# Rearranging the two front halves of an encoder layer: a gates piece moved to the short attention, two query heads to a bank, the second picks among gathers, the first query products ahead of the last transposes

## The chip, the cores and the metric

One NeuronCore of a Trainium2 chip runs the whole kernel in one launch. The metric is the device time of one execution in microseconds (us), and of several executions the median. The engines are TensorE (PE: matrix products and transposes; PEld in the profile is its loading of weights, which overlaps), VectorE (DVE), ScalarE (ACT), GpSimd (POOL) and SyncE (SP, which here only issues transfers).

## The reference

One encoder layer is computed for two sequences with the same weights: a prompt of 256 tokens, called "p" in the kernel, and a sample of 512 tokens, called "s". Everything is fp32.

```python
h = rms_norm(x, norm1)
proj = h @ w_in                                  # 1024 -> 5120 columns
qa, ka, va, qb, kb, vb, ga, gb = split(proj)
ya = banded_attention(rope(qa), rope(ka), va, sink) @ w_o_a       # 8 heads, 2 kv heads
ob = softmax-weighted sum of three dilated attentions of 4 heads each
yb = ob @ w_o_b
x = x + (sigmoid(ga) * ya + sigmoid(gb) * yb) @ w_out
t = rms_norm(x, norm2)                           # then the expert part, "peer"
q = (t @ w_query).reshape(T, 8 heads, 2, 128)
s1, s2 = scores of q against 128 + 128 sub-keys of each head
top 16 of s1, top 16 of s2, top 16 of their 256 sums  -> idx (128 experts a token), g
x = x + sum_e g_e * gelu(expert_u[idx_e] . t) * expert_v[idx_e]   # of 16384 experts
```

## The kernel before

**Products.** fp32 operands are split into two parts (`hi`, made by a cast on ScalarE, and `lo`, the rest, made by a subtraction on VectorE or GpSimd: `split`), and each product is three matmuls into the same bank of PSUM (`mm3`: hi by hi, hi by lo, lo by hi). Weights come through `w_stream` in pairs of 128x512 blocks: 512 KB into `wraw` (two buffers, issued by SP), a cast to `whi`, a subtraction to `wlo` (three buffers each). The table `LP` says which pairs are subtracted on GpSimd (`onpool`).

**The front of a sequence** (`front`), of nt = 2 tiles of 128 tokens for p and 4 for s, is in order: the norm and its transposes (`norm1`); six chunks of `w_in` (chunk c = 4 first, then 0, 1, 2, 3, 5), after each of which `post` norms and rotates queries and keys on VectorE and transposes them (`p_qk`), running along the next chunk's products; the attention (`att`), with 8 + 4 + 4 heads per tile; `merge`, which transposes the attention's outputs `on` (`p_toT<-ident,on`, split into `oTh` and `oTl`) and multiplies by `w_o_a` and `w_o_b` (`pya`, `pyb`); `w_out` (`pwo`, whose second half runs in two halves of the tiles, `proj_halves`); per tile `done`: the residual add, the norm, and the transposes of `xn` into `tTh` and `tTl` (`to_T`); and four chunks of `w_query` (`pq`, four heads of 128 columns each), whose results are copied (`qT`), scored against the keys (`p_s`) and reduced to the 16 best by `top16` on VectorE. The first query chunk of s is done for tokens 0:256 first and then for 256:512.

**Fillers.** The sigmoid gates' columns of `w_in` are computed in eight pieces (`PIECES`, `gates_pre`: for s 96 matmuls `pg` of 128x256 and two transfers of 512 KB a piece), and they fill the attention, where TensorE would wait for softmaxes. `along(att(), more, rate)` deals a piece's steps out among the attention's. In p's attention the filler `more` is s's first norm, p's own eight pieces, and those s pieces that `GS` puts there; `GS` also puts some behind p's `w_out`, and the rest fill s's attention.

**The prompt's experts** run beside everything else. `front("p")` runs alone. Then `fill(front("s"), gg, ...)` advances a chain `gg` by FILL = 2.25 steps for each unit that the front yields (a yield's number of units is written in the code; `IPW` is that of a pair of weights of s's projection, `MU` that of the other projections). The chain begins with the prompt's picks, `pick`, 11 steps for each of two tiles: candidates, 16 top-8 searches, and four rounds of `eq`, `pr`, `ex` (a compare, a product and a sum of 1600 elements a partition) on VectorE, ending in the table of expert numbers `pidx`. Then come the gathers, `gather`: for each tile 128 steps over `expert_u` and 128 over `expert_v`, in each of which GpSimd issues a transfer of 128 rows of 4 KB by `pidx` into `gr` and VectorE takes one product with it (`gr<-gr,tok` or `x<-gr,act,x`). There are 512 such steps. They go on beside the sample's dense expert part: `stage1` (all 16384 `expert_u` products, `pu`), `gbuild` (the sample's gates), `stage2` (all `expert_v` products, `held`). What is left of the chain at the end is run by itself.

**What sets the order.** Within an engine the instructions stand in an order that a scheduler writes down before the run, by priorities that follow the order in which the code issues them; where it expects a wait, it takes what comes later. On the chip each engine runs its list in order. So a step that the code moves takes with it everything that the scheduler places around it. The PSUM banks of the front are in four pairs: `mm` and `mb` for products (a `half` of 0 or 1), `tr` and `o` for transposes and attention outputs.

## Time and profile before

| | before |
|---|---|
| median of three runs | 2438.69 us (2438.09 to 2441.15) |
| the profiled execution: own time, span | 2441.6 us, 2439.8 us |
| TensorE busy, mean granted clock | 2332.6 us (96% of the span), 0.981 |
| VectorE busy | 1880.8 us (77%) |
| ScalarE busy | 1073.6 us (44%) |
| GpSimd busy | 830.0 us (34%) |

The profile is of one execution; the span runs from its first to its last instruction, and its own time is 1.8 us more. A wait is shown as the idle time ahead of an instruction, with the instruction that ended it. The granted clock is that of TensorE as a share of full speed. Names such as `wlo` or `gr` are the tiles of the code, with their numbers left out. Instructions of a front's helper all have the helper's line: L145 to L147 are the three matmuls of `mm3`, L243 to L245 those of a gates piece, L166 the transposes of `to_T`, L141 the subtraction of `split`, L813 the gather's product over `expert_u`, L821 that over `expert_v`.

### The profile page before, as it was taken

What the parts mean: (1) busy time and instruction counts of PE and PEld (TensorE: products, weight loads), DVE (VectorE), ACT (ScalarE), POOL (GpSimd) and SP (SyncE); (2) the same over time, 40 slices, a digit from 0 to 9 for tenths busy, and PEclk for the clock granted to TensorE, in tenths of its full rate; (3) what the DMA queues carried; (4) which work ended last, traced back from release to release, by engine and by line L of the source; (5) the groups of instructions that cost most, each with busy time, mean ns of one, the idle gap of its engine ahead of it and who ended that gap; (6) DMA issues with size and microseconds to landing.
All of it is one profiled execution on the core that took longest, in us unless ns stands there. A gap on an engine that the chain in (4) does not pass through costs nothing.

```text
span 2439.8 us, 34171 instructions
## 1 busy us (share of the span) xinstructions
PE 2332.6 (96%) x11926; PEld 1958.4 (80%) x11926; DVE 1880.8 (77%) x4013; ACT 1073.6 (44%) x1848; POOL 830.0 (34%) x624
## 2 busy tenths in 40 slices
PE   7998998999997999999999999998899999999996
PEld 5787986877977888888888888887688888888885
DVE  6765699687698889978577888771588787878787
ACT  5664444543433334366466667642333232222231
POOL 0000320255555500145244444440333344444443
PEclk9999999999998999999999999999899999999998
DMA  6423542477788434479789999893999999999997
GB/s 214 149 87 121 181 136 70 147 231 221 274 301 268 130 109 136 153 271 345 282 294 337 323 337 363 336 341 129 389 373 348 357 355 370 350 334 395 353 363 265
DMA packets 246365, 642.79 MB, mean 263 GB/s; under 512 B 22576, under 2 KB 77488, under 8 KB 244144
## 3 DMA queue, kind: packets, MB, share of 16 engines
q1 hardware_dynamic: 151728, 305.02, 36.7%
q0 software_dynamic: 73728, 268.47, 30.5%
q10 hardware_dynamic: 20736, 67.12, 6.9%
q8 instruction: 94, 1.54, 0.3%
q14 instruction: 79, 0.65, 0.1%
HBM read 561.60 MB, written 77.59 MB: 262 GB/s over the span
## 4 chain that ended last, share of the span: by engine, by line
PE 77%; DMA 8%; DVE 7%; issue 3%; ACT 2%; POOL 2%; SPq 0%; POOLq 0%; ACTq 0%; DVEq 0%
PE held L145 10%; PE held L146 9%; PE held L147 9%; PE pu L147 9%; PE pu L146 9%; PE pu L145 9%; PE p_g L725 5%; DMA wraw<-w_in 3%; DMA gr<-u,pidx 2%; PE pg L245 1%; PE pg L244 1%; DVE wlo L141 1%; POOL wlo L141 1%; PE pg L243 1%; ACT whi L140 1%
## 5 line engine op out<-in xcount | busy, mean ns | idle before, releaser
L806 POOL DMA_INDIRECT gr<-u,pidx x256 | 329.7, 1288 | 588.2 <-ACT ph L140 262.8
L806 POOL DMA_INDIRECT gr<-v,pidx x256 | 353.4, 1381 | 462.6 <-ACT ph L140 187.7
L145 PE MATMUL held<-vh,ph 128*128 128x512 f32 x1024 | 399.1, 391 | 17.5 <-ACT ph L140 17.5
L813 DVE SCALAR_TENSOR_TENSOR gr<-gr,tok 128x1024 f32<-128x1024 f32 x256 | 331.1, 1300 | 103.3 <-DMA gr<-u,pidx 103.2
L145 PE MATMUL pu<-tTh,uh 128*128 128x512 f32 x1024 | 406.2, 397 | 0.7 <-ACT uh L140 0.7
L147 PE MATMUL pu<-tTh,ul 128*128 128x512 f32 x1024 | 398.9, 390 | 0.6 <-DVE ul L141 0.6
L146 PE MATMUL pu<-tTl,uh 128*128 128x512 f32 x1024 | 399.2, 390 | 0.0
L146 PE MATMUL held<-vl,ph 128*128 128x512 f32 x1024 | 397.9, 390 | 0.0
L821 DVE SCALAR_TENSOR_TENSOR x<-gr,act,x 128x1024 f32<-128x1024 f32 x256 | 328.2, 1282 | 68.2 <-DMA gr<-v,pidx 66.4
L147 PE MATMUL held<-vh,pl 128*128 128x512 f32 x1024 | 332.4, 389 | 0.0
L141 POOL TENSOR_TENSOR wlo<-wraw,whi 128x1024 fp32r<-128x1024 f32 x51 | 126.0, 2472 | 376.0 <-ACT whi L140 369.2
L141 DVE TENSOR_TENSOR vl<-vr,vh 128x1024 fp32r<-128x1024 f32 x128 | 156.2, 1223 | 113.2 <-ACT vh L140 112.8
L145 PEld LDWEIGHTS held<-vh,ph 128*128 128x128 f32 x1024 | 193.2, 189 | 58.2 <-ACT ph L140 18.1
L140 ACT CAST uh<-ur 128x1024 fp32r<-128x1024 f32 x128 | 134.3, 1050 | 238.9 <-PE pu L146 127.4
L147 PEld LDWEIGHTS pu<-tTh,ul 128*128 128x128 f32 x1024 | 192.5, 188 | 41.3 <-DVE ul L141 1.1
L146 PEld LDWEIGHTS held<-vl,ph 128*128 128x128 f32 x1024 | 192.8, 188 | 40.2
L147 PEld LDWEIGHTS held<-vh,pl 128*128 128x128 f32 x1024 | 192.2, 188 | 40.0
L145 PEld LDWEIGHTS pu<-tTh,uh 128*128 128x128 f32 x1024 | 192.9, 188 | 38.3 <-ACT uh L140 1.1
L146 PEld LDWEIGHTS pu<-tTl,uh 128*128 128x128 f32 x1024 | 192.8, 188 | 37.2
L140 ACT CAST ph<-gl 128x512 fp32r<-128x512 f32 x128 | 79.5, 621 | 314.1 <-DVE gl L763 183.0
L140 ACT CAST whi<-wraw 128x1024 fp32r<-128x1024 f32 x137 | 143.7, 1050 | 160.7 <-DMA wraw<-w_in 54.4
L140 ACT CAST vh<-vr 128x1024 fp32r<-128x1024 f32 x128 | 134.2, 1050 | 176.5 <-PE held L147 98.4
(400 smaller groups left out, 4558.1 us busy)
## 6 DMA issues: line engine op xcount, KB each, us to landing
ur<-ublk SPq DMA_DIRECT2D x128, 512.0 KB, 4.6
vr<-v SPq DMA_DIRECT2D x128, 512.0 KB, 8.3
wraw<-w_in SPq DMA_DIRECT2D x80, 512.0 KB, 3.7
gd<-gs ACTq DMA_DIRECT2D x16, 2048.0 KB, 12.2
gt<-gd SPq DMA_DIRECT2D x16, 2048.0 KB, 17.1
gl<-ad SPq DMA_DIRECT2D x128, 256.0 KB, 8.6
wraw<-w_query SPq DMA_DIRECT2D x32, 512.0 KB, 4.0
wraw<-w_out SPq DMA_DIRECT2D x16, 512.0 KB, 4.4
```

Of the source, the lines that this page charges most:

```text
L140: i = ac.copy(hi, src)
L141: eng.tensor_tensor(lo, src, hi.bitcast(F32), op=ALU.subtract)
L145: a_ = pe.matmul(out, lhsT=lh, rhs=rh, start=first, stop=False)
L146: b_ = pe.matmul(out, lhsT=lh, rhs=rl, start=False, stop=False)
L147: c_ = pe.matmul(out, lhsT=ll, rhs=rh, start=False, stop=last)
L243: pe.matmul(o, lhsT=Th[:, kt, c], rhs=hi[:, j, :], start=(kt == 0 and t % 2 == 0), stop=False)
L244: pe.matmul(o, lhsT=Th[:, kt, c], rhs=lo[:, j, :], start=False, stop=False)
L245: pe.matmul(o, lhsT=Tl[:, kt, c], rhs=hi[:, j, :], start=False, stop=(kt == KT - 1 and t % 2 == 1))
L725: pe.matmul(p[:, j * 128:(j + 1) * 128], lhsT=o1[:, q % 8 + j, :], rhs=o2, start=True, stop=True)
L806: st = gp.indirect_dma_start(out=g, out_offset=None, in_=tab, in_offset=bass.IndirectOffsetOnAxis(ap=pidx[t][:, s:s + 1], axis=0))
L813: ve.scalar_tensor_tensor(g, g, 1.0, tok, op0=ALU.mult, op1=ALU.mult, accum_out=act[:, s:s + 1])
L821: ve.scalar_tensor_tensor(xt, g, act[:, s:s + 1], xt, op0=ALU.mult, op1=ALU.add)
```

## The change

- `GS` goes from (0, 1) to (1, 2). Before, the filler of p's attention held no s piece, piece 0 stood behind p's `w_out`, and seven pieces filled s's attention. Now piece 0 is in p's attention, piece 1 behind p's `w_out`, and six are left for s's attention.
- The prompt's query chunks put two heads (256 columns each) into one bank, two banks a chunk, and consecutive chunks alternate between the pairs `mm` and `mb`. Before, each of the four heads had a bank of its own.
- `IPW` goes from 0.4 (and 1.0 for chunk 4) to 0.52 (and 0.7). With seven gates pieces becoming six in s's attention, the sum of units of s's front goes from 57.0 to 56.2, that is from 128 to 126 steps of the chain: 22 steps of picks in both, 106 gather steps before and 104 now. `FG`, which had the same value as FILL, goes.
- The chain takes the first tile's picks, then the second tile's picks with five gather steps of the first tile among them, and then the rest.
- In s, the transposes of the second norm's tiles 2 and 3 are issued after the first query chunk's products for tokens 0:256, and a dependency holds them behind the last of these. These products go by heads 0 and 1, then 2 and 3. The last pair of that chunk's weights has its buffer in the norm's pool, so that it needs no free buffer of the stream.

```diff
FILL = 2.25
-FG = 2.25
...
-GS = (0, 1)
+GS = (1, 2)
 LP = (0, 2, 2, 1, 2, 1, 0)
-IPW = 0.4
+IPW = (0.7, 0.52)
...
-    def to_T(src, hi, lo, k0, n, col, natural=0):
+    def to_T(src, hi, lo, k0, n, col, natural=0, after=None):
...
-                pe.transpose(p[:, j * 128:(j + 1) * 128], src[:, (k + j) * 128:(k + j + 1) * 128], ident)
+                tr = pe.transpose(p[:, j * 128:(j + 1) * 128], src[:, (k + j) * 128:(k + j + 1) * 128], ident)
+                if after is not None:
+                    tc.add_manual_dep(tr.ins, after.ins.name, ORDERED, reason="products first")
...
             if last is not None and k == kts - 2:
-                hi = last.tile([128, 2, 512], F32R, tag="xhi", name="xhi", bufs=1)
-                lo = last.tile([128, 2, 512], F32R, tag="xlo", name="xlo", bufs=1)
+                hi = last[0].tile([128, 2, 512], F32R, tag=last[1] + "hi", name="xhi", bufs=1)
+                lo = last[0].tile([128, 2, 512], F32R, tag=last[1] + "lo", name="xlo", bufs=1)
...
-                    acc = yield from along(proj(fp, w_in[:, c * 512:(c + 1) * 512], KT, Th, Tl, nt, "pin", LP[0] if seq == "p" else LP[1] if c in (4, 0) else LP[6], 1.0 if c == 4 else IPW), rest, 0 if seq == "p" and c == 4 else 1)
+                    acc = yield from along(proj(fp, w_in[:, c * 512:(c + 1) * 512], KT, Th, Tl, nt, "pin", LP[0] if seq == "p" else LP[1] if c in (4, 0) else LP[6], IPW[c != 4]), rest, 0 if seq == "p" and c == 4 else 1)
...
                         norm_tok(np_, x[t0 + t], g2, xn, sq2[t][:, 0:1])
...
-                        to_T(xn, Th, Tl, 0, KT, t * 128)
-
+                        if seq == "s" and t >= 2:
+                            late.append((t, xn))
+                        else:
+                            to_T(xn, Th, Tl, 0, KT, t * 128)
+
+                    late = []
...
                     if seq == "p":
                         yield from gates_pre(PIECES[GS[0]:GS[1]], tTh, tTl, 4, put_s)
+                    else:
+
+                        first = [ps_mm(f"pq{m}", m // 2) for m in range(4)]
+                        got = list(w_stream(a["w_query"][:, 0:512], KT, LP[5], (np_, "y")))
+                        for ms in ((0, 1), (2, 3)):
+                            for kt, hi, lo in got:
+                                for m in ms:
+                                    mc = slice(m * 128, m * 128 + 128)
+                                    p3 = mm3(first[m][:, 0:256], hi[:, mc], lo[:, mc], Th[:, kt, 0:256], Tl[:, kt, 0:256], kt == 0, False)
+                        for t, xn in late:
+                            to_T(xn, Th, Tl, 0, KT, t * 128, after=p3[2])
+                        for kt, hi, lo in got:
+                            for m in range(4):
+                                mc = slice(m * 128, m * 128 + 128)
+                                mm3(first[m][:, 256:512], hi[:, mc], lo[:, mc], Th[:, kt, 256:512], Tl[:, kt, 256:512], False, kt == KT - 1)
...
             for c in range(4):
-                acc = [ps_mm(f"pq{m}", m // 2) for m in range(4)]
-
-                parts = [slice(0, 256), slice(256, 512)] if c == 0 and seq == "s" else [slice(0, S)]
-                ws = w_stream(a["w_query"][:, c * 512:(c + 1) * 512], KT, LP[2] if seq == "p" else LP[5], pp if len(parts) > 1 else None)
-                got = []
-                for i, cp_ in enumerate(parts):
-                    for kt, hi, lo in got if i else ws:
-                        if i == 0 and len(parts) > 1:
-                            got.append((kt, hi, lo))
+                if seq == "p":
+
+                    two = [ps_mm("pq", c % 2) for _ in range(2)]
+                    acc = [two[m // 2][:, m % 2 * 256:m % 2 * 256 + 256] for m in range(4)]
+                elif c == 0:
+                    acc = first
+                else:
+                    acc = [ps_mm(f"pq{m}", m // 2) for m in range(4)]
+                if seq == "p" or c:
+                    for kt, hi, lo in w_stream(a["w_query"][:, c * 512:(c + 1) * 512], KT, LP[2] if seq == "p" else LP[5]):
                         for m in range(4):
                             mc = slice(m * 128, m * 128 + 128)
-                            mm3(acc[m][:, cp_], hi[:, mc], lo[:, mc], Th[:, kt, cp_], Tl[:, kt, cp_], kt == 0 and i == 0, kt == KT - 1 and i == len(parts) - 1)
+                            one = seq == "p"
+                            mm3(acc[m][:, 0:S], hi[:, mc], lo[:, mc], Th[:, kt, :], Tl[:, kt, :],
+                                kt == 0 and not (one and m % 2), kt == KT - 1 and not (one and m % 2 == 0))
...
     run(front("p"))
-    def picks_p():
-        for t in range(2):
-            yield from pick(pks["p"][1], "p", t, *tops["p"][t])
+    def gathers():
+
+        yield from pick(pks["p"][1], "p", 0, *tops["p"][0])
+        g0 = gather(gpl, 0)
+        for i, _ in enumerate(pick(pks["p"][1], "p", 1, *tops["p"][1])):
+            yield 1
+            if i % 2:
+                next(g0)
+                yield 1
         pks["p"][0].__exit__(None, None, None)
-        tops_done[0] = 1
-
-    tops_done = [0]
-    gg = chain(picks_p(), gather(gpl, 0), gather(gpl, 1))
-    fill(front("s"), gg, (FILL, FG))
+        yield from g0
+        yield from gather(gpl, 1)
+
+    gg = gathers()
+    fill(front("s"), gg, FILL)
```

The scheduled order, which the diff does not tell, changes at these places. First, TensorE at the end of p's attention, from the last softmax's transposes (`p_PT`) to the first product with `w_o_a` (`pya`); `pg` is a gates piece, of p where it reads `pTl` and of s where it reads `tTh` or `tTl`. Before:

```order
L447 MATMUL p_PT<-ident,sm 128x128 x2
L245 MATMUL pg<-whi,pTl 128x256
L166 MATMUL p_toT<-ident,on_176 128x128 x4
L454 MATMUL oB<-V_183,PT 128x64 x4
L447 MATMUL p_PT<-ident,sm 128x128 x2
L166 MATMUL p_toT<-ident,on_176 128x128 x2
L454 MATMUL oB<-V_183,PT 128x64 x2
L166 MATMUL p_toT<-ident,on_177 128x128 x6
L145 MATMUL pya_2097<-whi,oTh 128x512
```

And now:

```order
L244 MATMUL pg<-whi,tTh 128x256
L245 MATMUL pg<-wlo,tTh 128x256
L246 MATMUL pg<-whi,tTl 128x256
L165 MATMUL p_toT<-ident,on_176 128x128 x6
L165 MATMUL p_toT<-ident,on_177 128x128 x6
L144 MATMUL pya_2213<-whi,oTh 128x512
```

Nothing stood between the last attention product (`oB`) and the transposes of the second tile's output; now 53 products of the moved piece stand there, and the transposes of both tiles follow in one block.

Second, TensorE at the end of s's attention, from the filler's last products to the first product with `w_o_a`. Before:

```order
L245 MATMUL pg<-whi,tTl 128x256
L166 MATMUL p_toT<-ident,on_3423 128x128 x2
L166 MATMUL p_toT<-ident,on_3424 128x128 x6
L166 MATMUL p_toT<-ident,on_3425 128x128 x4
L243 MATMUL pg<-whi,tTh 128x256
...
L245 MATMUL pg<-whi,tTl 128x256
L166 MATMUL p_toT<-ident,on_3425 128x128 x2
L166 MATMUL p_toT<-ident,on_3426 128x128 x6
L145 MATMUL pya_7102<-whi,oTh 128x512
```

And now:

```order
L244 MATMUL pg<-whi,tTh 128x256
L245 MATMUL pg<-wlo,tTh 128x256
L246 MATMUL pg<-whi,tTl 128x256
L165 MATMUL p_toT<-ident,on_3531 128x128 x6
L165 MATMUL p_toT<-ident,on_3532 128x128 x6
L165 MATMUL p_toT<-ident,on_3533 128x128 x6
L165 MATMUL p_toT<-ident,on_3534 128x128 x6
L144 MATMUL pya_7091<-whi,oTh 128x512
```

Before, 156 products of gates pieces stood behind the last attention product, 95 of them between the transposes of the third tile; now there are 25, all ahead of the transposes, and the 24 transposes of the four tiles stand together.

Third, VectorE among the picks, where chunk 4's fourth tile is normed (`nat<-nat,rs_r` 128x128), rotated (the `r` rows) and written (`nat<-r,r`), beside the second tile's picks. Before:

```order
L674 TENSOR_TENSOR eq<-posx,tf 128x1600
L398 TENSOR_TENSOR nat<-r_3850,r_3851 128x2x16
L135 TENSOR_TENSOR rs_t<-rs_t,rs_v 128x8
L387 SCALAR_TENSOR_TENSOR rs_r<-rs_r,rs_t 128x2
L129 TENSOR_SCALAR rs_v<-ssq 128x8
L676 TENSOR_TENSOR pr<-eq,ce 128x1600
L136 TENSOR_SCALAR rs_t<-rs_t 128x8
L388 TENSOR_TENSOR nat<-nat,rs_r 128x128
L132 RECIPROCAL rs_r<-rs_r 128x8
L677 TENSOR_REDUCE ex<-pr 128x32
L674 TENSOR_TENSOR eq<-posx,tf 128x1600
```

And now:

```order
L389 TENSOR_TENSOR nat<-nat,rs_r 128x128
L131 RECIPROCAL rs_r<-rs_r 128x8
L699 TENSOR_TENSOR pr<-eq,ce 128x1600
L657 TENSOR_TENSOR pw_88<-pw_88,gsm 128x128
L388 SCALAR_TENSOR_TENSOR rs_r<-rs_r,rs_t 128x8
L396 TENSOR_TENSOR r_4010<-nat,rck_norm_a 128x32
L397 TENSOR_TENSOR r_4011<-nat,rsk_norm_a 128x2x8
L398 TENSOR_TENSOR r_4011<-nat,rsk_norm_a 128x2x8
L133 TENSOR_TENSOR rs_t<-rs_r 128x8
L836 SCALAR_TENSOR_TENSOR gr,act<-gr,tok 128x1024
L700 TENSOR_REDUCE ex<-pr 128x32
L697 TENSOR_TENSOR eq<-posx,tf 128x1600
```

From the end of the first tile's picks (the cast to its `pidx`) to the last add of that fourth tile's rotation (`nat<-r,r` 128x2x16), VectorE had three `eq`, three `pr` and two `ex` of the second tile's picks to do; now it has two `eq`, one `pr`, one `ex` and the first gather's product, and this product stands four small rows behind the first `pr`. At the other end of the program, behind the last add of the sample's output, VectorE has 14 gather products to do where it had 12.

## Rows read from the trace of the kernel before

**Rows 1.** Page, part 1: busy us, share and instructions by engine.
```profile
PE 2332.6 (96%) x11926; PEld 1958.4 (80%) x11926; DVE 1880.8 (77%) x4013; ACT 1073.6 (44%) x1848; POOL 830.0 (34%) x624
```

**Rows 2.** Windows: stretch, its length, busy time by engine, PE clock, DMA share.
```profile
175.00:200.00 25.00, 20.69 (x140) 18.48 (x140) 13.35 (x38) 13.73 (x28) 0.00 (x0) 0.93 0.23 79
...
350.00:375.00 25.00, 17.67 (x74) 13.42 (x72) 24.83 (x81) 8.69 (x15) 3.17 (x9) 0.94 0.39 112
375.00:400.00 25.00, 21.45 (x82) 16.88 (x83) 25.00 (x59) 9.13 (x18) 0.00 (x0) 0.86 0.12 31
...
750.00:775.00 25.00, 15.09 (x66) 12.68 (x65) 21.77 (x53) 10.68 (x21) 14.97 (x11) 0.72 0.92 307
1750.00:2400.00 650.00, 650.00 (x2869) 538.08 (x2868) 527.94 (x663) 191.22 (x237) 265.47 (x207) 1.00 0.97 359
```

**Rows 3.** Timeline of PE at the end of p's attention: start, us, [idle before].
```profile
194.31 1.54 PE L166 MATMUL p_toT<-ident,on 128*128 128x128 f32 x6 [4.01 <-DVE pb L532]
```

**Rows 4.** Timeline of POOL, last weight subtractions of p's query.
```profile
306.77 2.40 POOL L141 TENSOR_TENSOR wlo<-wraw,whi 128x1024 fp32r<-128x1024 f32 x1 [5.23 <-ACT whi L140]
314.68 2.35 POOL L141 TENSOR_TENSOR wlo<-wraw,whi 128x1024 fp32r<-128x1024 f32 x1 [5.51 <-ACT whi L140]
```

**Rows 5.** Timeline of PE where s's projection starts.
```profile
316.94 0.71 PE L611 MATMUL p_s<-kys,qT 128*128 128x128 f32 x4 [1.69 <-ACT qT L608]
317.41 0.48 PE L145 MATMUL pin<-whi,tTh 128*128 128x512 f32 x1
```

**Rows 6.** Waits of PE from 300 to 450 us: total, times, longest.
```profile
PE pin L146 <- DVE wlo L141: 6.3, 3, 2.8
PE pin L145 <- ACT nat L422: 3.7, 3, 1.6
PE p_qk L401 <- DVE rs_t L134: 2.5, 1, 2.5
```

**Rows 7.** Timeline of VectorE among the picks.
```profile
376.72 1.82 DVE L676 TENSOR_TENSOR pr<-eq,ce 128x1600 f32<-128x1600 bf16 x1
...
379.68 1.81 DVE L677 TENSOR_REDUCE ex<-pr 128x32 f32<-128x1600 f32 x1
381.40 0.98 DVE L674 TENSOR_TENSOR eq<-posx,tf 128x1600 bf16<-128x1600 bf16 x1
```

**Rows 8.** DMA issues from 470 to 800 us: median us from issue to landing.
```profile
gr<-u,pidx POOLq DMA_INDIRECT x101, 5.6
```

**Rows 9.** Timeline of VectorE, a gather's product and its wait.
```profile
452.20 1.23 DVE L813 SCALAR_TENSOR_TENSOR gr<-gr,tok 128x1024 f32<-128x1024 f32 x1 [3.44 <-DMA gr<-u,pidx]
```

**Rows 10.** PE by line from 649.7 to 669.6 us: busy, mean ns, idle before.
```profile
L243 PE MATMUL pg<-whi,tTh 128*128 128x256 f32 x52 | 14.8, 286 | 0.0
```

**Rows 11.** Timeline of PE at the start of s's output projections.
```profile
671.85 0.50 PE L145 MATMUL pya<-whi,oTh 128*128 128x512 f32 x1 [1.26 <-ACT oTh L140]
...
674.44 0.74 PE L147 MATMUL pya<-whi,oTl 128*128 128x512 f32 x2 [1.39 <-DVE oTl L141]
```

**Rows 12.** Waits of VectorE from 640 to 672 us: total, times, longest.
```profile
DVE gr L813 <- DMA gr<-u,pidx: 10.5, 5, 2.8
```

**Rows 13.** Timeline of PE at the start of s's query.
```profile
763.65 1.94 PE L166 MATMUL p_toT<-ident,xn 128*128 128x128 f32 x8 [6.61 <-DVE rs_t L136]
767.32 1.94 PE L166 MATMUL p_toT<-ident,xn 128*128 128x128 f32 x8 [1.73 <-DVE xn L157]
...
771.87 0.58 PE L146 MATMUL pq<-tTl,whi 128*128 128x256 f32 x1 [1.57 <-DVE tTl L141]
```

**Rows 14.** Timeline of all engines in s's second norm.
```profile
754.10 0.15 DVE L566 TENSOR_TENSOR sq<-sq 128x1 f32<-128x1 f32 x1
...
758.75 2.51 POOL L141 TENSOR_TENSOR wlo<-wraw,whi 128x1024 fp32r<-128x1024 f32 x1
...
759.00 2.29 DVE L566 TENSOR_TENSOR sq<-sq 128x1 f32<-128x1 f32 x1
```

**Rows 15.** Timeline of VectorE at the end.
```profile
2420.16 15.80 DVE L821 SCALAR_TENSOR_TENSOR x<-gr,act,x 128x1024 f32<-128x1024 f32 x12
```

4 lines of the change are left out of this document (2 added, 2 removed).

## Prediction

> **What bounds the kernel now.** I read the page's first part, then the windows, then the waits and the timeline of the stretches that the change touches. TensorE is busy 2332.6 of 2439.8 us, far more than any other engine [rows 1], and in the long stretch from 1750 to 2400 us it never stands still, at a granted clock of 1.00 [rows 2]. So an engine that is made lighter elsewhere gains nothing; time can be won only where TensorE waits, and such a win is kept to the end, since all that follows moves forward with it. The waits lie in the fronts. The windows show four stretches of 25 us with 15 to 21 us of work [rows 2]: the end of p's attention (20.69), the picks beside s's projection (17.67 and 21.45), and s's second norm (15.09). In all four the granted clock is under 1.00, down to 0.72, so the work there also runs partly at the lower of the two levels (1.2 GHz, not 2.4): a wait costs a little more than its own length. Each part of the change is aimed at one of these places, and I price them one by one against this execution's own time of 2441.6 us, which is 2.9 above the median of the runs.
>
> **A. The gates piece in p's attention.** Before the second tile's transposes TensorE waits 4.01 us for the attention's last arithmetic on VectorE [rows 3], with nothing in the order to fill it. Now 53 matmuls of the piece stand there. What they take is read from the same kind elsewhere: three groups of 52, so 156, pass in the 19.9 us from 649.7 to 669.6 with no idle time ahead of them [rows 10], 0.128 us each with some transposes included. 53 of them are 6.8 us, more than the wait. The piece's 96 matmuls are not new, they leave s's attention, so the gain is the wait: **-4.0**. Its two transfers of 512 KB go to SP's queue in a stretch whose DMA share is 0.23 [rows 2], beside other work. Against it: the transposes of both tiles now follow each other, and the first product with `w_o_a` must wait for a cast of the first; the same kind of wait in s was 1.26 [rows 11]. So -2.7 is the low end; the high end is -4.0.
>
> **B. Two query heads to a bank in p.** The next chunk need no longer wait for four copies out of its banks. But that is not what sets the pace: GpSimd's subtractions come every 7.9 us for two pairs of weights [rows 4], 15.8 us for a chunk, while a chunk's 96 matmuls of 256 columns are 12.3 us at 0.128, and some scores. Only where the stream ends does the copy show: TensorE waits 1.69 us for `qT` at 316.94, and s's first product follows at 317.41, when the subtraction that began at 314.68 and took 2.35 is done (317.03) [rows 4, 5]. I take **-1.7**, between nothing (the stream was the bound throughout) and -3.4 (the same wait in one more place). The price of sharing a bank, that a head's copy waits for its neighbour's last products, is a few matmuls of 0.128.
>
> **C. The picks.** From 300 to 450 us TensorE waits 6.3 us for `wlo` from VectorE, 3.7 for the buffers `nat` and 2.5 for a norm, 12.5 in all [rows 6], while VectorE is busy for all of 375 to 400 us [rows 2]: it has picks to do, in pieces of 1.82 (`pr`), 1.81 (`ex`) and 0.98 (`eq`) [rows 7], and chunk 4's small norms queue between them. The order says what changes: up to the fourth tile's rotation three `eq`, three `pr` and two `ex`, 12.0 us, become two, one and one with a gather's product of 1.23 [rows 9], 6.8 us. Everything behind it (the next chunk's `nat`, its `wlo`) comes 5.2 us earlier. What it costs is the first gather. Its transfer can start when `pidx` is cast, and lands 5.6 us later by the median [rows 8]; the product stands one `eq`, one `pr` and some small rows behind that cast, about 4.0 us, so VectorE stands for 1.6. Sum **-3.6**. The bounds: -8.8 if the waits for `wlo` and the norm go altogether (6.3 + 2.5) [rows 6]; +11.2 if two gathers stall VectorE for a whole landing each (2 x 5.6) and nothing is won. That some picks come later in the program is hidden: only gathers need them. The units of `IPW` decide beside which products these steps fall; that is in the order already.
>
> **D. The end of s's attention.** This is what A takes away. With 156 gates matmuls behind the last attention product, the four tiles' transposes and their splits lay under other work, and TensorE's waits were 1.26 for `oTh` and 1.39 for `oTl` [rows 11]. Now 25 are left, 3.2 us, and the 24 transposes come as one block of eight groups in four banks: the fifth group waits until the first has been split. I price that as one more round of the same two waits, **+2.6**. The low end is 0 (the splits keep up). The high end is two gathers on VectorE ahead of the split, each with its product of 1.23 [rows 9] and the longest wait of this stretch, 2.8 [rows 12]: +8.
>
> **E. The transposes of s's second norm.** TensorE waits 6.61, 1.73 and 1.57 us here [rows 13]. The first is for the residual adds and the norm of tile 0, behind the same number of gathers in both orders, and stays. The second is for tile 1's `xn`: it now stands one gather and two adds earlier on VectorE, over 1.23 us, and I let the 1.73 go. Holding tiles 2 and 3 back behind 96 products (12.3 us) hides their norms, but then nothing is left between their transposes and the products that read them; the wait for such a split is the 1.57 of the third row. So -1.73 + 1.57 = **-0.2**. The bounds: -9.9 if all three go, +5 if the late norms are three gathers' waits late (3 x 1.6, by C).
> The row at 759.00 says what else can happen here: an addition of one element took 2.29 us while GpSimd subtracted a pair of weights from 758.75 for 2.51; the same instruction took 0.15 at 754.10 [rows 14]. The chunk's four pairs are still subtracted on GpSimd in this stretch, so a second such meeting would cost the chain 2.1. The Trainium skill's page SBUF — State Buffer, section "SBUF: two separate sides", gives the reason: VectorE and GpSimd share one pair of ports, and whoever comes second waits for the whole instruction. The trace agrees (2.29 against 0.15). By that rule this change is not safer than before, and with one more meeting E would be +1.9.
>
> **F. The end.** Behind the sample's last output VectorE takes 12 gather products in 15.80 us [rows 15], 1.32 each, and nothing else is left. Two fewer steps fall into s's front, and the order shows 14 here: **+2.6**. It could be nothing only if the last products found room earlier, which the order excludes.
>
> **Sum:** -4.0 - 1.7 - 3.6 + 2.6 - 0.2 + 2.6 = -4.3, that is 2437.3 for an execution like the profiled one, and 2434.4 against the median of 2438.69. A measurement of this kernel can tell 0.2%, 4.9 us, from no change; so this forecast lies just within "the same".
>
> **Rivals.**
> 1. *The waits go altogether.* C at -8.8, E at half of its 9.9 (-5.0), D at half (+1.3): -4.0 - 1.7 - 8.8 + 1.3 - 5.0 + 2.6 = -15.6, 2423.1. For it: VectorE's blocks of 1.8 us are what TensorE waits for in C, and the clock there (0.86 and 0.94) would come back too. Against it: VectorE has the same sum of work in that stretch and is full [rows 2].
> 2. *What is won is eaten at the end of s's attention.* D at +8: -4.0 - 1.7 - 3.6 + 8.0 - 0.2 + 2.6 = +1.1, 2439.8. For it: VectorE waited for gathers five times there, 10.5 us in all [rows 12], and the cover of 16.8 us of gates (131 x 0.128) is gone.
> 3. *Slower: the gathers among the picks stall VectorE in front of the norms.* C at +11.2: -4.0 - 1.7 + 11.2 + 2.6 - 0.2 + 2.6 = +10.5, 2449.2. It decides from the point where C is above +5.6, two waits of 2.8; a single wait of 3.44 has been seen [rows 9]. Against it: GpSimd has little to do there, so the transfers can start early.
>
> **How the numbers follow.** The forecast (2430 to 2439) gets 0.46, of which 0.21 lies under 2433.8; rival 1 0.22; rival 2 0.19, nearly all within 0.2%; rival 3 0.13, of which 0.10 lies above 2443.6. So faster 0.43, the same 0.45, slower 0.12. The range must hold eight in ten: half of rival 1 lies below its 2423.1, and some 0.09 of rival 3 above 2444, so it goes from 2423 to 2444. All the good bounds at once would lie below it and all the bad ones above it; several would have to fall together.
>
> **What would show it.** A: no idle time over 1.3 us ahead of the `p_toT<-ident,on` of p. B: `pq` and `pin` without a wait for `qT`. C: PE's waits for `wlo`, `nat` and the norm under 9 us in sum, and gathers from about 380 us with waits under 2 us; the first stall over 3.5 us on VectorE there speaks for rival 3. D: `p_toT<-ident,on` and `pya` of s with 4 to 6 us of waits; over 9 is rival 2. E: a block of 16 transposes, 96 products, 16 transposes, with a wait of 1.5 to 2 us behind the second. F: 14 products in some 18.4 us at the end. The prediction is wrong if the middle of the program, whose order I take as equal, gives back or adds more than the fronts do.

## The result and the profile after

The changed kernel is slower: 2460.02 us median of five executions (2453.89 to 2465.16), against 2441.15 for the kernel before, timed beside it (2438.09 to 2444.64). The ratio is 1.0069, 95% interval 1.0052 to 1.0085. The forecast was 2434.4 with a range up to 2444.

The profiled execution has a span of 2458.3 us, 18.5 more than before, and TensorE does the same work (the page's first part):

```profile
PE 2333.9 (95%) x11926; PEld 1957.4 (80%) x11926; DVE 1882.6 (77%) x4013; ACT 1068.2 (43%) x1846; POOL 812.8 (33%) x624
```

So the difference is idle time and clock. I cut both traces at the same events of the program (the first `pq` of p, the first and last `pin` of s, its last `oB`, its first `pya`, `pwo`, `pq` and `pu`) and asked for the windows between. The changed kernel's rows (stretch, length, busy time of PE, PEld, DVE, ACT, POOL, PE clock, DMA share, GB/s):

```profile
0.00:262.83 262.83, 243.65 (x1430) 201.93 (x1431) 169.55 (x423) 149.69 (x274) 13.39 (x11) 0.99 0.48 150
262.83:318.83 56.00, 52.43 (x434) 51.66 (x433) 34.34 (x182) 23.01 (x41) 17.53 (x8) 1.00 0.53 173
318.83:482.79 163.96, 147.46 (x657) 117.50 (x656) 146.59 (x555) 71.29 (x129) 27.26 (x31) 0.97 0.38 118
482.79:665.58 182.79, 175.00 (x1169) 142.44 (x1168) 131.08 (x319) 75.97 (x213) 91.55 (x69) 0.95 0.68 215
665.58:684.84 19.26, 7.96 (x55) 7.08 (x53) 13.15 (x21) 7.15 (x13) 9.17 (x8) 0.74 0.91 334
684.84:719.55 34.71, 33.65 (x155) 27.63 (x156) 25.68 (x37) 14.72 (x24) 13.76 (x10) 1.00 0.81 288
719.55:784.93 65.38, 51.08 (x231) 41.44 (x229) 52.18 (x81) 18.68 (x34) 35.97 (x25) 0.92 0.77 258
784.93:897.68 112.75, 108.84 (x624) 96.45 (x624) 82.50 (x443) 35.55 (x55) 41.65 (x21) 0.97 0.37 118
```

Four of the rows of the kernel before, s's projection, its attention, the way to the first `pya`, and `w_out` with the norm:

```profile
317.41:475.10 157.69, 144.84 (x655) 117.30 (x653) 137.62 (x530) 70.56 (x126) 22.30 (x27) 0.97 0.37 111
475.10:649.10 174.00, 169.35 (x1139) 137.30 (x1138) 130.09 (x312) 75.55 (x212) 96.29 (x68) 0.97 0.70 221
649.10:671.85 22.75, 21.49 (x182) 21.25 (x180) 11.48 (x24) 11.96 (x21) 11.26 (x8) 1.00 1.01 382
708.14:769.08 60.94, 50.11 (x225) 40.48 (x224) 50.64 (x78) 20.45 (x36) 36.85 (x26) 0.93 0.85 283
```

The same cut of both, idle being the length less PE's busy time, and the clock's loss that busy time by what the clock is short of 1.00 (it has two digits, so half a per cent of the stage is rounding):

| stage | length before | after | idle before | after | clock's loss before | after |
|---|---|---|---|---|---|---|
| p, to its first query product | 260.18 | 262.83 | 25.1 | 19.2 | 4.7 | 2.4 |
| p's query | 57.23 | 56.00 | 4.1 | 3.6 | 0 | 0 |
| s's projection | 157.69 | 163.96 | 12.9 | 16.5 | 4.3 | 4.4 |
| s's attention, to the last `oB` | 174.00 | 182.79 | 4.7 | 7.8 | 5.1 | 8.8 |
| from there to the first `pya` | 22.75 | 19.26 | 1.3 | 11.3 | 0 | 2.1 |
| merge | 36.29 | 34.71 | 1.4 | 1.1 | 0 | 0 |
| `w_out` and norm | 60.94 | 65.38 | 10.8 | 14.3 | 3.5 | 4.1 |
| s's query | 110.75 | 112.75 | 2.1 | 3.9 | 4.3 | 3.3 |

The 96 products moved from s's attention to p's lengthen the first stage by some 11.5 us (0.12 each) and shorten the fourth and fifth together by as much. The first stage grew by only 2.65: it won 8.9. (A stage of one profile is not exact: with the old `GS` this one is 255.4 to 261.9 us long in seven kernels, 258.5 in the mean, and with the new one 261.2 to 264.6 in thirteen, 262.3 in the mean. By the means it won some 8.) Of the later stages of s only the merge did not lose. After the first `pu` the rest is 2.1 us shorter up to the last dense product (1537.7 to 1535.6) and 2.7 longer behind it. Read with the work moved back, s's projection lost 6.3, its attention with the way to `pya` 16.8 (the length 5.3 longer, with 11.5 less to do), `w_out` 4.4, the query 2.0.

**The place that lost most.** TensorE's timeline after the last attention product answers to [rows 11]:

```profile
670.33 0.87 PE L165 MATMUL p_toT<-ident,on 128*128 128x128 f32 x6 [0.49 <-DVE pb L533]
...
681.77 2.82 PE L165 MATMUL p_toT<-ident,on 128*128 128x128 f32 x12 [10.57 <-DVE oTl L140]
684.84 0.55 PE L144 MATMUL pya<-whi,oTh 128*128 128x512 f32 x1 [0.25 <-ACT oTh L139]
```

Half of the 24 transposes stop for 10.57 us, for the subtraction `oTl` that frees a bank. VectorE in that time:

```profile
671.39 0.41 DVE L534 TENSOR_TENSOR on<-pb,es 128x256 f32<-128x256 f32 x1
675.21 1.22 DVE L836 SCALAR_TENSOR_TENSOR gr<-gr,tok 128x1024 f32<-128x1024 f32 x1 [3.40 <-DMA gr<-u,pidx]
...
678.31 2.80 DVE L836 SCALAR_TENSOR_TENSOR gr<-gr,tok 128x1024 f32<-128x1024 f32 x1 [1.87 <-DMA gr<-u,pidx]
...
681.04 1.94 DVE L140 TENSOR_TENSOR oTl<-p_toT,oTh 128x512 fp32r<-128x512 f32 x4
```

Between the last attention output at 671.39 and the first `oTl` at 681.04 stand two gather products. They waited 3.40 and 1.87 us for their rows, and the second took 2.80 where 1.22 is usual, while GpSimd subtracted a pair of weights:

```profile
677.67 2.35 POOL L140 TENSOR_TENSOR wlo<-wraw,whi 128x1024 fp32r<-128x1024 f32 x1
```

9.2 us for two products. Nothing was left for TensorE to do meanwhile.

**The same at the second norm** (TensorE, then VectorE), to be read beside [rows 13]:

```profile
781.22 3.27 PE L165 MATMUL p_toT<-ident,xn 128*128 128x128 f32 x16 [11.73 <-DVE xn L156]
```

```profile
775.49 3.41 DVE L836 SCALAR_TENSOR_TENSOR gr<-gr,tok 128x1024 f32<-128x1024 f32 x1 [3.21 <-DMA gr<-u,pidx]
```

This product stands between the two halves of the norms of tiles 0 and 1, and holds both for 6.6 us.

**In the attention** the stops are short, but the longest is followed by the lower level of the clock. TensorE waits 2.56 us, and then for some 20 us the windows show a clock of 0.76, 0.50 and 0.88, with PE busy for all of 560 to 580 (timeline, then windows):

```profile
554.90 0.66 PE L475 MATMUL sB<-qk 64*128 64x384 f32 x1 [2.56 <-DVE st L477]
```

```profile
550.00:560.00 10.00, 7.44 (x37) 6.04 (x38) 7.94 (x15) 2.87 (x8) 6.23 (x5) 0.76 0.76 260
560.00:570.00 10.00, 10.00 (x31) 6.11 (x31) 4.13 (x10) 1.79 (x5) 1.42 (x3) 0.50 0.49 159
570.00:580.00 10.00, 10.00 (x71) 8.92 (x71) 7.05 (x17) 4.20 (x11) 4.65 (x5) 0.88 0.68 195
```

That is 2.4, 5.0 and 1.2 us of clock (the windows' length by what the clock is short of 1.00), 8.6 in all, behind a wait of 2.56: nearly the whole 8.8 of this stage. Behind the stage's other stops, up to 1.39 us, the clock stays at 1.00; in the kernel before it fell for shorter behind stops of 1.04 and 2.16 us.

**What went as forecast.** At the end of p's attention the wait of [rows 3] is gone, with 0.80 us for a cast in its place, and at the program's end 14 products stand where [rows 15] show 12:

```profile
200.17 1.48 PE L165 MATMUL p_toT<-ident,on 128*128 128x128 f32 x12
202.45 0.50 PE L144 MATMUL pya<-whi,oTh 128*128 128x512 f32 x1 [0.80 <-ACT oTh L139]
```

```profile
2435.94 18.45 DVE L844 SCALAR_TENSOR_TENSOR x<-gr,act,x 128x1024 f32<-128x1024 f32 x14
```

### The profile page after: what moved, and what is told of

Same layout as the page of the kernel before. It is cut to its first block, busy times and chain, and to the rows that moved or that the text cites. A ratio compares the mean times of both kernels' runs of the same rounds, so it can differ in the third digit from the quotient of the medians.

```text
span 2458.3 us, 34168 instructions
## 1 busy us (share of the span) xinstructions
PE 2333.9 (95%) x11926; PEld 1957.4 (80%) x11926; DVE 1882.6 (77%) x4013; ACT 1068.2 (43%) x1846; POOL 812.8 (33%) x624
## 4 chain that ended last, share of the span: by engine, by line
PE 69%; DVE 10%; DMA 9%; issue 7%; POOL 3%; ACT 2%; SPq 0%; POOLq 0%; ACTq 0%; DVEq 0%
PE held L144 9%; PE held L145 9%; PE held L146 9%; PE pu L146 9%; PE pu L144 9%; PE pu L145 9%; PE p_g L748 4%; DMA gr<-u,pidx 3%; DMA wraw<-w_in 3%; POOL gr L829 2%; POOL wlo L140 2%; DVE wlo L140 1%; DVE x L844 1%; ACT whi L139 1%; DVE gr L836 1%
## 5 line engine op out<-in xcount | busy, mean ns | idle before, releaser
L829 POOL DMA_INDIRECT gr<-u,pidx x256 | 318.6, 1245 | 628.4 <-ACT ph L139 271.9
L836 DVE SCALAR_TENSOR_TENSOR gr<-gr,tok 128x1024 f32<-128x1024 f32 x256 | 338.0, 1325 | 94.2 <-DMA gr<-u,pidx 94.0
L844 DVE SCALAR_TENSOR_TENSOR x<-gr,act,x 128x1024 f32<-128x1024 f32 x256 | 328.3, 1283 | 58.4 <-DMA gr<-v,pidx 56.2
## 6 DMA issues: line engine op xcount, KB each, us to landing
gd<-gs ACTq DMA_DIRECT2D x16, 2048.0 KB, 10.6
```

The source lines that it names most:

```text
L829: st = gp.indirect_dma_start(out=g, out_offset=None, in_=tab, in_offset=bass.IndirectOffsetOnAxis(ap=pidx[t][:, s:s + 1], axis=0))
L836: ve.scalar_tensor_tensor(g, g, 1.0, tok, op0=ALU.mult, op1=ALU.mult, accum_out=act[:, s:s + 1])
L844: ve.scalar_tensor_tensor(xt, g, act[:, s:s + 1], xt, op0=ALU.mult, op1=ALU.add)
```

## The experiments

Theory 1: the moved piece was the cover of the attention outputs' transposes, and its absence is the loss. Theory 2: gather products that stand on VectorE and wait for late rows stop the softmaxes, splits and norms that TensorE waits for, and the change put more of them in front of these. Rivals stand in the expectations. Each run gives its ratio to the kernel before, timed on the same chip.

**One part alone, or one part undone.** First the gates piece alone, and the change without it.

```diff
-GS = (0, 1)
+GS = (1, 2)
```

> The kernel before with only the gates piece moved (GS (1, 2)). Theory 1, the piece was the cover of the attention outputs' transposes: p's front wins about 9 us over the 11.5 us of added products, as in the changed kernel (its first query product only 2.65 us later), but the wait for oTl in s's merge appears, some 8 to 10 us, and the end grows by four gather products (16 where 12 were, 5.3 us). Sum +4 to +7 over before. Rival, the picks and units are the cause: the merge shows the old waits of 2.6 us, and the sum is -9 + 5 = -4.

Measured: 0.9999 (0.9982 to 1.0016). In its profile p's stage is as in the changed kernel (263.00 us) and the wait ahead of `p_toT<-ident,on` in s is 5.90 us; 16 products stand at the end. The wait appears as theory 1 says, smaller than its 8 to 10, but the balance is even, better than it forecast.

```diff
-GS = (1, 2)
+GS = (0, 1)
```

> The changed kernel with the gates piece put back (GS (0, 1)). Theory 1: 96 products stand among the transposes of s's attention outputs again and the wait of 10.6 us there is gone; p's front loses its 9 us; the end has 10 products where 14 were, 5.3 us less. Sum about -6 to -7 against the changed kernel, so some +11 over before is left to the other parts. Rival, the piece has no share in the loss: the time rises by the 9 us of p's front and falls by 5 at the end, +4 against the changed kernel.

Measured: 1.0039 (1.0021 to 1.0058). The wait for `oTl` is gone, as expected; s's attention is still 185.6 us long at a clock of 0.93. So the piece costs nothing on the kernel before and some 0.3% on top of the other parts, and 0.39% is lost without it.

```diff
-        yield from pick(pks["p"][1], "p", 0, *tops["p"][0])
-        g0 = gather(gpl, 0)
-        for i, _ in enumerate(pick(pks["p"][1], "p", 1, *tops["p"][1])):
-            yield 1
-            if i % 2:
-                next(g0)
-                yield 1
+        for t in range(2):
+            yield from pick(pks["p"][1], "p", t, *tops["p"][t])
         pks["p"][0].__exit__(None, None, None)
-        yield from g0
+        yield from gather(gpl, 0)
```

> The changed kernel with the second picks ahead of all gathers again, the units kept. Theory 1 holds that the interleaving is a small part: s's projection, 6.3 us longer in the changed kernel, changes by less than 3 us, and the wait at the merge stays at 8 to 11 us. Rival, the gathers among the picks stall VectorE and so cost the projection: it is 6 us shorter, and the sum -6 against the changed kernel.

Measured: 1.0060 (1.0040 to 1.0080). s's projection took 159.19 us, 4.8 less than in the changed kernel, more than theory 1 allowed and near to what the rival said, but the attention was 3.1 longer, the wait for `oTl` 10.6 again, and the time is not told from the changed kernel's.

```diff
-                        if seq == "s" and t >= 2:
+                        if False:
...
-                elif c == 0:
-                    acc = first
+                elif c == 0:
+                    acc = [ps_mm(f"pq{m}", m // 2) for m in range(4)]
...
```

> The changed kernel with the transposes of the second norm's tiles 2 and 3 in their old place. Theory 1: the wait ahead of the first transposes of xn, 11.7 us in the changed kernel against 6.6, comes from gathers that land late on VectorE ahead of the norm, not from the new order, so it stays between 8 and 12, and the sum moves by less than 3 us. Rival, the new order is the cause: the wait falls back to 6 to 7 us and the stretch from w_out to the first expert product is 4 to 6 us shorter.

Measured: 1.0063 (1.0040 to 1.0087). `w_out` and the norm have 14.0 us of idle time, as in the changed kernel (14.3), 11.2 of it ahead of the transposes of `xn`. The late transposes are not the cause of that wait.

```diff
-IPW = 0.4          # and 1.0 for chunk 4
+IPW = (0.7, 0.52)
```

> The kernel before with only the units of s's projection changed (0.7 and 0.52 for 1.0 and 0.4). Theory 2, added after the first four runs: the units move the gather steps against the attention, VectorE meets more late gathers among the softmaxes, TensorE stops a little longer and its clock is granted at the lower level for longer. So this alone is slower, by 6 to 10 us, with s's attention 6 us or more longer at a granted clock under 0.96. Rival, the units are harmless and the loss comes with the picks among gathers, the bank or the late transposes: within 3 us of before.

Measured: 1.0028 (1.0013 to 1.0043), slower, so the units are not harmless. The size is within theory 2's 6 to 10 (6.9 by the medians), but only in part where it said: the attention was 178.9 us at a clock of 0.97, 4.9 longer, `w_out` 65.5 against 60.9, and s's query 114.7 against 110.8. (The picks among gathers have no run of their own: with the old units the second tile's picks would still hold their memory when the attention needs it. That was not tried.)

```diff
 # the changed kernel with the old units and the old order of picks
-IPW = (0.7, 0.52)
+IPW = (1.0, 0.4)
```

> The changed kernel with the units and the picks put back, so that gates piece, shared bank and late transposes are left. Theory 2: without the units the loss in s's attention (granted clock 0.95 in the changed kernel, 0.97 before) is gone, and what is left is the even balance of the gates piece: within 4 us of before, some 13 to 17 under the changed kernel. Rival: still 8 us or more above before.

Measured: 1.0025 (1.0009 to 1.0041), between the two. The attention has 174.1 us at 0.98, as theory 2 says, but 0.25% stays.

```diff
-                    two = [ps_mm("pq", c % 2) for _ in range(2)]
-                    acc = [two[m // 2][:, m % 2 * 256:m % 2 * 256 + 256] for m in range(4)]
+                    acc = [ps_mm(f"pq{m}", m // 2) for m in range(4)]
...
-                            one = seq == "p"
+                            one = False
```

> The changed kernel with a bank for each head of the prompt's query again. The bank's own gain was priced at 1.7 us and the price of sharing at nothing: so the sum is 0 to 3 us above the changed kernel. Rival: sharing costs something downstream (gates, bank and late transposes were 6 us slower than before where the gates alone were even), and the sum falls by 3 us or more.

Measured: 1.0064 (1.0038 to 1.0089), not told from the changed kernel. p's query took 59.6 us against 56.0, so the bank wins its 1.7 and more there, but s's projection took 158.8 against 164.0. What the bank wins in one stage is lost in the next (the two windows):

```profile
261.65:321.28 59.63, 55.14 (x439) 53.93 (x437) 39.17 (x200) 25.22 (x44) 19.24 (x8) 0.97 0.51 164
321.28:480.07 158.79, 145.26 (x654) 117.33 (x653) 141.19 (x536) 70.83 (x126) 27.84 (x30) 0.97 0.39 122
```

For the next, the kernel before with the edits of only_gates and the late transposes together:

> The kernel before with the gates piece moved and the late transposes, without the bank, the units and the picks. If the late transposes cost the 6 us that gates, bank and late transposes together lost against the gates alone, this is 4 to 8 us over before. If the bank did, it is even with before, like the gates alone.

Measured: 1.0017 (1.0006 to 1.0027), 3.6 us by the medians, just under the 4 to 8 of the first case. No single part holds the rest.

**Fewer gather steps in the attention.** In the changed kernel, and in the kernel before with the gates piece (0.36 and 0.53 there):

```diff
-AT, GP = (0.45, 0.5)
+AT, GP = (0.3, 0.5)
...
-                    yield 0       # s's query, once a head
+                    yield 0.68
```

> The changed kernel with fewer gather steps dealt out in s's attention: a head counts 0.30 for 0.45, the gates pieces left after the last head count nothing, and s's query deals out 0.68 units a head instead; about as many steps as before in all. The gathers ahead of the splits of the attention outputs in VectorE's order fall from nine to five. If the gathers that land late in front of softmaxes and splits are the cause, the attention is 6 to 10 us shorter, the wait for oTl is under 5 us, and the sum is 10 us or more under the changed kernel. If the missing cover alone is the cause, the wait for oTl stays at 8 us or more.

Measured: 1.0052 (1.0031 to 1.0072). Where the steps were thinned it went as theory 2 says: the attention 164.9 us with 1.6 of idle time at a clock of 1.00, 18 less than in the changed kernel (5.8 of them are 48 products that moved behind the last `oB`), and a wait for `oTl` of 2.62. But the sum fell by some 4 us and not by 10: the merge took 9.8 more, and in s's query the steps stood ahead of the first expert weights, for which TensorE now waited:

```profile
886.46 0.80 PE L144 MATMUL pu<-tTh,uh 128*128 128x512 f32 x1 [6.26 <-ACT uh L139]
890.94 0.80 PE L146 MATMUL pu<-tTh,ul 128*128 128x512 f32 x1 [3.25 <-DVE ul L140]
```

> The kernel before with the gates piece moved and the gather steps thinned in s's attention (0.36 for 0.45, the left pieces nothing, s's query 0.53 a head). If late gathers eat what the piece wins in p's front (about 9 us), this gives the gain back: faster than before by 4 to 8 us though 17 products stand at the end where 12 stood (6.6 us). If not, it is 5 us slower than before, by the end alone.

Measured: 1.0055 (1.0038 to 1.0073), slower than the gates piece alone, with a wait of 7.22 us for the same `ul`. A step that is put elsewhere is paid there.

**No waiting for landings.** The first attempt read a fixed tile (and the gathers' own buffers go from three to two, which is not shown):

```diff
-            ve.scalar_tensor_tensor(g, g, 1.0, tok, op0=ALU.mult, op1=ALU.mult, accum_out=act[:, s:s + 1])
+            ve.scalar_tensor_tensor(still, still, 0.0, tok, op0=ALU.mult, op1=ALU.mult, accum_out=act[:, s:s + 1])
```

> The changed kernel, but the first tile's 128 products over expert_u read (and overwrite with zeros) one fixed tile and not the gathered rows, so the prompt's output is not the reference's; the transfers run as before into two buffers, and VectorE does as many products of the same size. No product waits for a landing. Theory 2 (late landings on VectorE stop the softmaxes, splits and norms that TensorE waits for): s's attention at a granted clock of 0.98 or more with under 4 us of idle time, the wait for oTl under 4 us, w_out's idle time down by 4 us or more, and the sum 15 us or more under the changed kernel. Theory 1 (the cover is missing) alone: the wait for oTl stays at 8 us or more and the sum falls by less than 6.

> The same edit in the kernel before: the first tile's products over expert_u read one fixed tile. By theory 2 it gains too, but less than the changed kernel does, so that the changed kernel without landings is no more than 5 us from the kernel before without landings, where with them it is some 17 behind. If the loss has another cause, the distance stays above 12.

Measured: 1.0388 (1.0362 to 1.0414) and 1.0395 (1.0368 to 1.0421). Both failed as experiments: without a need for `pidx` the scheduler drew the products into s's projection, where VectorE in the second of these kernels had 68 of them from 320 to 545 us (by line):

```profile
L833 DVE SCALAR_TENSOR_TENSOR still<-still,tok 128x1024 f32<-128x1024 f32 x68 | 85.0, 1250 | 0.0
```

The second attempt keeps them near their places by an order dependency on the transfer, which no engine waits for (cut: the line that keeps the transfer, and the other branch):

```diff
-            ve.scalar_tensor_tensor(g, g, 1.0, tok, op0=ALU.mult, op1=ALU.mult, accum_out=act[:, s:s + 1])
+            if t == 0:
+                pr = ve.scalar_tensor_tensor(tok, tok, 0.0, tok, op0=ALU.mult, op1=ALU.mult, accum_out=act[:, s:s + 1])
+                tc.add_manual_dep(pr.ins, issued[0].ins.name, ORDERED, reason="place")
```

> The changed kernel; the first tile's products over expert_u read and write their own token tile (times zero, so the prompt's output is not the reference's) and not the gathered rows, with an order dependency on the transfer that keeps them near their places; the transfers run as before and nothing on VectorE waits for them. Theory 2 (late landings): s's attention at a granted clock of 0.97 or more, the wait for oTl and the clock loss behind it at most half of the changed kernel's 10.6 and 5.0 us, w_out's idle time down by 4 us or more, and the sum 12 us or more under the changed kernel. Theory 1 (cover and places): the wait for oTl stays over 8 us, and the sum falls by less than 6.

> The same edit in the kernel before. By theory 2 it gains less than the changed kernel, 3 to 8 us, and the distance between the two shrinks from 17 to under 7 us. If the landings cost both alike, it gains as much as the changed kernel, and the distance stays.

Measured: the changed kernel 0.9904 (0.9888 to 0.9919), the kernel before 0.9930 (0.9914 to 0.9946); 2418.90 and 2424.13 us. This pair bears most on the theories. Without landings the changed kernel is 5.2 us faster than the one before, and the landings cost it 41 us (2460.02 less 2418.90) where they cost the other 18 (2442.37 less 2424.13). The second figure is more than the 3 to 8 that were expected, and the distance between the two not only shrinks but changes its sign. Windows of the attention, the way to `pya`, and (last) `w_out` with the norm, in the kernel before without landings and in the changed one without:

```profile
473.22:638.64 165.42, 165.42 (x1158) 136.20 (x1157) 132.68 (x327) 77.08 (x213) 101.30 (x70) 1.00 0.75 239
638.64:660.00 21.36, 19.43 (x163) 18.98 (x161) 14.15 (x21) 12.21 (x22) 13.70 (x10) 1.00 0.98 364
...
694.12:751.25 57.13, 50.78 (x231) 41.76 (x229) 55.44 (x84) 19.91 (x35) 40.49 (x27) 0.97 0.87 302
```

```profile
478.95:638.38 159.43, 159.43 (x1196) 136.71 (x1195) 134.15 (x327) 77.62 (x214) 98.18 (x70) 1.00 0.78 252
638.38:649.62 11.24, 4.18 (x30) 3.30 (x28) 11.24 (x19) 6.46 (x12) 6.63 (x5) 0.73 0.98 344
...
689.19:748.75 59.56, 50.68 (x231) 41.69 (x229) 56.48 (x85) 20.21 (x36) 36.53 (x25) 0.92 0.85 289
```

In the attention TensorE is busy for the whole stretch, at a clock of 1.00, in both. On the way to `pya` 7.1 us of idle time are left in the changed kernel, against 11.3 with landings and 1.9 in the kernel before. The waits for `oTl` are 6.0 of them, more than the half of 10.6 that theory 2 allowed, so theory 1's missing cover has a share. It can't be read off as 7.1: here no gates product is left behind the last `oB`, where 25 stand with landings, and TensorE's longer wait is for a gather product that stands ahead of the split and took 3.53 us beside a subtraction on GpSimd (TensorE, VectorE, GpSimd):

```profile
647.06 1.54 PE L165 MATMUL p_toT<-ident,on 128*128 128x128 f32 x6 [3.51 <-DVE oTl L140]
```

```profile
642.86 3.53 DVE L839 SCALAR_TENSOR_TENSOR tok<-tok 128x1024 f32<-128x1024 f32 x1
```

```profile
642.95 2.36 POOL L140 TENSOR_TENSOR wlo<-wraw,whi 128x1024 fp32r<-128x1024 f32 x1
```

The edit changes a little more than the waiting. A transfer no longer waits for VectorE to free its buffer (the DMA share in the attention is 0.75 and 0.78, with landings 0.70 and 0.68), and some products moved: 60 of them lie in s's attention in both kernels, where 55 and 56 do with landings, and fewer in s's query.

**Issuing the gathers earlier.** GpSimd's issue of a gather waits for a buffer and for the latest pacing instruction on ScalarE. The second kind is, from 480 to 800 us, before and after (total, times, longest):

```profile
POOL gr L806 <- ACT sm L443: 17.1, 13, 4.5
```

```profile
POOL gr L829 <- ACT sm L444: 37.2, 19, 4.9
```

```diff
-            if anchor[0] is not None:
+            if anchor[0] is not None and not (t == 0 and tab is a["u"]):
                 tc.add_manual_dep(st.ins, anchor[0].ins.name, SYNC, reason="pace")
```

> before_gv without the pacing dependency for the first tile's gathers over expert_u. If the pacing makes the landings late, VectorE's waits for gr (52.8 us from 320 to 800 before) fall by a third or more, and the sum is 3 to 8 us under before_gv. If the buffers set the pace, the waits and the sum stay within 3 us.

> The changed kernel without that pacing and with 1.85 steps a unit in the last stage. The end gives back 16 to 18 us (14 products). If the pacing is what delayed its gathers, s's attention loses its 7.8 us of idle time and 9 of clock as well, and the sum is 25 us or more under the changed kernel and even with before_gv or faster. If not, it is 16 to 18 under the changed kernel, 8 to 12 us slower than before_gv.

Measured: 1.0089 (1.0070 to 1.0107) and 1.0150 (1.0127 to 1.0173), slower by far, against both expectations. VectorE's waits for `gr` from 320 to 800 us fell to 36.6 us in the first, from 52.8 before (54.4 in before_gv), about the third that the theory of late issue expects; in the second they fell to 40.4 from 58.0, but s's attention kept some 9 us of idle time. And the gathers moved forward into s's projection, where VectorE has no room: 195.00 us at a clock of 0.91 where before_gv has 158.09, with 182.0 of them busy on VectorE. The pacing keeps that stage free. Whether its doubled wait for `sm` is a cause of the changed kernel's loss stays open.

```profile
319.73:514.73 195.00, 156.10 (x641) 121.94 (x641) 182.01 (x604) 69.22 (x123) 80.74 (x74) 0.91 0.67 213
```

**Clearing the end.**

```diff
-GB, GV = (2.3, 1.75)
+GB, GV = (2.3, 1.85)
```

> The kernel before with the gates piece moved, and 1.85 for 1.75 gather steps a unit in the last dense stage, so that two products stand behind the last output where 16 stood. If the gates piece is even only because of four more products at the end, and the dense stage takes the steps without a wait of TensorE (none from 1750 to 2400 us before), this is 12 us or more under only_gates and some 0.4 to 0.7% faster than before. If the transfers (DMA share 0.97 there) don't keep up, TensorE waits in the dense stage, and the gain is under 4 us.

> The kernel before with 1.85 for 1.75 gather steps a unit in the last dense stage, so that no product stands behind the last output where 12 stood (15.8 us). If the end is all that it changes, it is 10 to 15 us faster than before, and faster than gates_gv. If gates_gv won by the gates piece, this is even with before.

Measured: with the gates piece 0.9980 (0.9965 to 0.9995), less than the 0.4 to 0.7% that were asked, and without it 0.9956 (0.9941 to 0.9972), as expected. So the four products more at the end were not what held the gates piece at even: with two products left at the end it is some 0.2% behind, though the intervals touch. The kernel before with 1.85 is the fastest that computes everything, 2431.09 us against 2442.37. Its last gather products stand ahead of the eight output adds:

```profile
2407.25 6.57 DVE L836 SCALAR_TENSOR_TENSOR x<-gr,act,x 128x1024 f32<-128x1024 f32 x5
2413.73 5.30 DVE L804 TENSOR_TENSOR xe<-held,xe 128x512 f32<-128x512 f32 x8
```

TensorE waits 3.0 us from 1750 to 2400 where it did not wait, so of 15.8 us at the end some 11 are kept.

## Why the prediction was wrong

**A** was right in kind and too small: the first stage won 8.9 here and some 8 by the mean of all profiles, not 4.0. Idle time fell by 5.9, and the clock's loss by 2.3, which I had not priced.

**B** (-1.7): p's query is 1.2 shorter, and 3.6 shorter than in no_bank. That the price of sharing is "a few matmuls" was wrong: s's projection pays, as C shows, and both stages together take 220.0 us with the bank and 218.4 in no_bank.

**C** (-3.6) failed at the step "everything behind it comes 5.2 us earlier". I had counted VectorE's rows from the cast of the first `pidx` on, and taken that cast at its old time. It moved from 373.47 to 381.59, while s's first product moved by 1.4 us. Before, and now:

```profile
373.47 0.21 DVE L681 CAST pidx<-ex 128x128 int32<-128x128 f32 x1
```

```profile
381.59 0.21 DVE L704 CAST pidx<-ex 128x128 int32<-128x128 f32 x1
```

The units, which make chunk 4 count less, are not the reason. With them alone (only_units) the cast stands where it stood:

```profile
372.85 0.21 DVE L696 CAST pidx<-ex 128x128 int32<-128x128 f32 x1
```

It goes with the shared bank. In the changed kernel, no_gates, no_picks, no_late, gates_bank_late, thin and nowait_after, which have it, the cast comes 61.5 to 63.6 us behind s's first product, and TensorE has one wait of 5.8 us for `wlo`. In the kernel before, only_gates, only_units, gates_late, gates_thin, no_bank, nowait_before, before_gv and gates_gv, which do not, it comes 53.7 to 56.3 us behind, and no wait for `wlo` in s's projection is over 2.8. A likely reason, not shown: p's query ends sooner, with VectorE busy 34.3 us in it instead of 37.5, and what VectorE has not done goes into the next stage. The wait in the changed kernel:

```profile
375.82 0.79 PE L145 MATMUL pin<-wlo,tTh 128*128 128x512 f32 x1 [5.81 <-DVE wlo L140]
```

TensorE's waits of [rows 6] are now

```profile
PE pin L145 <- DVE wlo L140: 8.0, 4, 5.8
PE pin L144 <- ACT nat L423: 3.5, 4, 1.3
...
PE p_qk L402 <- DVE rs_t L134: 1.3, 1, 1.3
```

with smaller ones 15.3 in all from s's first product on, where I asked for under 9; the stage lost 6.3. The gathers among the picks, my rival 3, have a share: with the bank and the old order of picks (no_picks, gates_bank_late) s's projection takes 159.2 us, with the bank and the new order (the changed kernel, no_gates, no_late, thin) 162.3 to 164.1, and in the changed kernel without landings 160.5. That is 3 to 5 us, not the two whole landings that the rival priced; the first of these gathers waited 1.14 us.

**D**, with the attention ahead of it, is the step with the largest error: +2.6, with +8 as the high end, where the attention and the way to `pya` lost 16.8. The wait for `oTl` alone is 10.57, and with the clock (0.74 in that stretch) the way to `pya` lost some 12. I priced one round of the old waits. The two gather products ahead of the split took 9.2 us, which is rival 2's place, its mechanism and about its price (two gathers, +8). Missing cover and landings both have a share in the 11.3 us of idle time; how large each is stays open, since the nowait runs leave 7.1 with still less cover.

**What no term held** is the attention itself. I took its order as unchanged but for the piece. It lost 3.1 us of idle time and 3.7 of clock before the last `oB`, and both are gone where nothing waits for landings (0.00 idle at 1.00). The part of the clock hangs on one stop of one profile; in the other kernels this stage has a clock of 0.93 to 1.00.

**E** (-0.2) lost 4.4. A gather product in the middle of the norms held them for 6.6 us; the late transposes are not the cause (no_late). Without landings the stage is still 2.4 us longer than in the other kernel (59.56 against 57.13), so the landings are a part of it and not all. **F** (+2.6) was right: 2.65.

With nothing waiting for landings the change is worth -5.2 us, where I had -4.3. That these are so close is luck: by the stages of the two nowait profiles A is -7.0 there, C +2.8, and everything behind the first `pu`, F included, -2.3. The sign came from the landings, 41 us against 18, nearly all of it ahead of the first `pu` (37.8 against 17.2 by the profiles). I had priced a product's wait for its row only in C and in D's high end. VectorE does not wait much longer for rows in the changed kernel; from 480 to 800 us, before and after (total, times, longest):

```profile
DVE gr L813 <- DMA gr<-u,pidx: 46.0, 39, 3.1
```

```profile
DVE gr L836 <- DMA gr<-u,pidx: 50.5, 35, 3.4
```

So what differs seems to be mainly what stands behind such a wait, as at the two places above; it was not counted for every place. That the landings turn the sign is shown by the nowait pair, within the limits said there. How they are shared among the parts is not: each part undone alone leaves 0.39 to 0.64%, the gates alone cost nothing, the units alone 0.28%, and these do not add up to 0.69% in any simple way. The thinned kernels and those without pacing suggest why: VectorE has to take these products somewhere, and each place has its own price.

## What to carry to other kernels

Price a reordering on the engine whose instructions wait for transfers, not only on the one that is full: for each place where the full engine waits, count the waiting rows that now stand ahead of what it waits for, and price each with its wait and with the clock behind it. An amount of work that covers a chain at one place is a cost when it is moved, and this cost can be as large as the gain at the new place. A stage that the full engine leaves sooner may hand unfinished work of another engine to the next stage, as seems to be so here with the bank, so a gain there is read over both. And when an interval between two events is counted from an order, read the time of the first event again in the new order before it is used.

## What was not expected of the hardware

A wait of 2.56 us of TensorE was followed by 8.6 us of lost clock (0.76, 0.50, 0.88 over 30 us) though it was then busy throughout; in the two kernels without landings, where TensorE never stands still in s's attention, the clock was 1.00 there. And the executions seem to differ more with the landings: without them five executions of the changed kernel lie between 2417.08 and 2419.93 us, with them between 2453.89 and 2465.16. For the kernel before it is less clear: six lie between 2422.08 and 2429.19 without, and the seventeen beside them between 2434.87 and 2447.53 with landings.
